# A decoder step on one core: a quarter of the first expert matrix loaded without a copy, and the residual's transposition of x taken from DRAM

## The chip, the core and the metric

The kernel runs on one core of a Trainium2 chip. The core has five engines with queues of their own: PE (TensorE, matrix products into PSUM), DVE (VectorE), ACT (ScalarE), POOL (GpSimd) and SP (SyncE, which here only issues DMAs). ACT and POOL issue DMAs too. Every DMA is served by the core's 16 DMA engines; the profile calls SP's queue q1, ACT's q10 and POOL's q0. The metric is the device time of one execution in microseconds (us), as the median of three runs.

## What is computed

The reference is one step of one layer for 256 prompt tokens and 64 sample tokens (T = 320 rows) of width D = 2048, all float32. What matters here:

```python
def layer(x, ...):
    m, ... = mixer(rmsnorm(x, norm_mix), ...)          # w_in, SSD scan, short convolution, w_out
    x = x + m                                          # x itself is needed again here
    x = x + mem_attend(rmsnorm(x, norm_mem_q), ...)
    x = x + peer(rmsnorm(x, norm_ffn), w_peer_q, sub_keys, peer_u, peer_v)

def rmsnorm(x, g):
    return x * rsqrt(mean(x * x) + EPS) * g            # a factor for each row, a gain for each column

# peer, in each block: all 16384 experts' rows of u and v are candidates
act = gelu(einsum('td,tkd->tk', xi, u[ei]))
out = einsum('tk,tkd->td', gi * act, v[ei])
```

The memory keys and values are `rmsnorm(mem) @ w_mem_k` and `@ w_mem_v`, for the prompt.

## The kernel before

**Stages.** PE's work is one long row of matrix products, stage after stage: memory keys and values (`tokens_gemm`, 8 column tiles of 16 units, lines 309 to 350), then w_in with the SSD scan worked in between (`gemm`, units of 12 products 128x320), the z part of w_in, w_out in two halves, memory attention, the retrieval scores, the first expert matrix u (`u_unit`, 128 tiles of four units) and the second, v (`v_unit`). Each weight tile is cut in a high and a low part, H and L (`split`, line 262: ACT copies to H, DVE subtracts for L), and three products of them replace one in full precision. Seven H and seven L tiles go round.

**Order of the work.** The orders on PE, ACT and DVE are those in which the program is written (`manual_schedule`); a stream (class `Stream`) runs loads, splits and products of successive units some steps apart: up to three loads ahead, and the split of a unit about six units ahead of its products. At each unit that leaves the stream ("a pop") side generators advance by a fixed rate: `strm.side(gen, rate)`. The orders on POOL and SP are set by the scheduler, which places instructions by its own estimate of when they are ready. In the expert stages POOL's order is written too.

**x for the mixer** (`norm_T`, lines 438 to 463). In the first stage a side generator (rate 0.36) loads x in three blocks of rows (128, 128, 64), takes the sum of squares on ACT, the row factor r, multiplies each row on DVE by r and by the gain, which was loaded as a broadcast tile of 1 MB (`gain_rows`), transposes four 128-column pieces at a time on PE, and splits the 512 columns into `AH` and `AL` in one ACT and one DVE instruction.

**x for the residual** (`residual`, lines 1071 to 1088). In the z part another side generator loads x again as rows (`xr`, POOL's queue), transposes it on PE in twelve groups of four, and ACT copies each group to `XF`. Beside it `short_in` (1090 to 1098) loads the short convolution's result `ys` back from DRAM on POOL's queue, 16 pieces into three buffers, and splits them into `BH` and `BL`. Behind both, POOL's queue has the first loads of memory keys, `kv` (line 1162).

**The first expert matrix.** A row of peer_u is wanted with 32-column blocks in an order that DVE's 32x32 transposition (line 2043) can use. So `ordered_rows` (586 to 597) copies peer_u in DRAM to `u_d`, 128 copies of 1 MB issued from ACT's queue in the early stages, at 0.12 and then 0.272 copies a pop; in the u stage `rows` (lines 2020 to 2025) loads a tile of 1 MB with one DMA in runs of 8 KB, into one of three rooms. A room falls free when DVE has transposed its last quarter. The same stage gathers rows of peer_u for the sample tokens, 1 MB a gather, on POOL's queue (`gu`, line 1925).

Of the kernel before, what the change touches and what calls it, by code (L numbers as in the profile page):

```python
# [11 lines left out]
F32 = mybir.dt.float32  # L12
# [3 lines left out]
AF = mybir.ActivationFunctionType  # L16
# [32 lines left out]
XW, LAG = 5, 4  # L49
AIN, AHEAD, HOT, G2B = 2, 1, 2, 3  # L50
Q_AHEAD, Q_ROOM, KV_MORE = 5, 4, 2

QA, QB = (0, 2, 4, 6, 8, 10, 12, 14, 15, 16), (0, 4, 6, 8, 9, 11, 13, 14, 15, 16)
QN = (QA, QB, QA)
# [111 lines left out]
def wait(n):  # L166
    for _ in range(n):
        yield 1
# [11 lines left out]
def step(ctx, tc, ins, outs, dbg=None, stop=None):  # L180
# [81 lines left out]
    def split(h, l, src):  # L262

        S.activation(h, src, AF.Copy)  # L264
        V.tensor_tensor(l, src, h.bitcast(F32), ALU.subtract)  # L265
# [141 lines left out]
    xh_d = drp.tile([D, TP], F32R, name="xh_d")  # L407
    xl_d = drp.tile([D, TP], F32R, name="xl_d")
    x1_d = drp.tile([P, KC, T], F32, name="x1_d")
    x2_d = drp.tile([TP, D], F32, name="x2_d")  # L410
    x2s_d = drp.tile([TS, D], F32, name="x2s_d")
    acc_d = drp.tile([P, 1024], F32, name="acc_d")
    act_d = drp.tile([P, P, TP], F32, name="act_d")
    u_d = [drp.tile([P, 4 * D], F32, name=f"u_d{i}") for i in range(P // 4)]
    g2_d = drp.tile([P, NG1 // 4, 4 * P], F32, name="g2_d")


# [12 lines left out]
    def rstd(st, n):  # L430
        V.tensor_scalar(st[:n, 1:2], st[:n, 0:1], 1.0 / D, EPS, op0=ALU.mult, op1=ALU.add)
        rsqrt(st[:n, 2:3], st[:n, 3:4], st[:n, 1:2])
        return st[:n, 2:3]
# [1 line left out]
    def tokens():  # L435
        return pM.tile([P, D], F32, tag="xt", bufs=2, name="xt")

    def norm_T(src, n, gb, h, l, cols):

        xt = tokens()  # L440
        nc.sync.dma_start(xt[:n], src)
        yield from wait(2)
        junk = pM.tile([P, D], mybir.dt.bfloat16, tag="junk", bufs=1, name="junk")
        st = pM.tile([P, 4], F32, tag="st", bufs=3, name="st")
        for i in range(2):
            half = slice(1024 * i, 1024 * i + 1024)
            S.activation(junk[:n, half], xt[:n, half], AF.Square, accum_out=st[:n, i:i + 1])
            yield 1
        V.tensor_tensor(st[:n, 0:1], st[:n, 0:1], st[:n, 1:2], ALU.add)
        r = rstd(st, n)  # L450
        yield 1
        for g in range(5):
            if g < 4:
                part = slice(512 * g, 512 * g + 512)
                V.scalar_tensor_tensor(xt[:n, part], xt[:n, part], r, gb[:n, part], ALU.mult, ALU.mult)
            if g:
                pt = ps("pt")
                for j in range(4):
                    k = 4 * g - 4 + j
                    transpose(pt[:, j * n:(j + 1) * n], xt[:n, k * P:(k + 1) * P])  # L460
                split(h[:, 4 * g - 4:4 * g, cols], l[:, 4 * g - 4:4 * g, cols],
                      pt[:, 0:4 * n].rearrange("p (j n) -> p j n", j=4))
            yield 1

    def gain_rows(g):
        gb = pM.tile([P, D], F32, tag="gb", bufs=1, name="gb")
        nc.sync.dma_start(gb, g.rearrange("(o d) -> o d", o=1).broadcast_to([P, D]))
        return gb


    gk = pM.tile([16, P], F32, name="gk")
# [43 lines left out]
    strm.side(mi, 0.75)  # L515

    def x_norm():
        yield from wait(2)
        gb = gain_rows(norm_mix[0])
        yield from wait(2)  # L520
        for b in range(2):
            yield from norm_T(x_prompt[0, b * P:(b + 1) * P], P, gb, AH, AL, slice(b * P, b * P + P))
        yield from norm_T(x_sample.rearrange("b l d -> (b l) d"), TS, gb, AH, AL, slice(TP, T))


    TRI = pX.tile([P, P], F32, name="TRI")
# [59 lines left out]
    def ordered_rows(share):  # L586
        pops = count()

        done_ = 0.0
        for i in range(P // 4):  # L590
            for b in range(4):
                while done_ < 1:
                    done_ += share[0] if next(pops) < 100 else share[1]
                    yield 1
                done_ -= 1
                nc.scalar.dma_start(u_d[i][32 * b:32 * b + 32].rearrange("p (a d) -> p a d", d=512),
                                    peer_u[0, 512 * i:512 * i + 512, 512 * b:512 * b + 512].rearrange("(a p) d -> p a d", p=32))

    strm.steady = chain(wait(36), ordered_rows((0.12, 0.272)))
    side = strm.side(chain(x_norm(), vectors(), histories()), 0.36)  # L600
    for w, dst in ((w_mem_k, p_mem_k), (w_mem_v, p_mem_v)):
        d2 = dst[0, 0].rearrange("m h d -> m (h d)")
        for c in range(4):
# [466 lines left out]

    def residual():

        xts = []
        for b in range(3):
            if b < 2:
                for src in (x_prompt[0, 0:P], x_prompt[0, P:TP]) if b == 0 else (x_sample.rearrange("b l d -> (b l) d"),):
                    xts.append(pZ.tile([P, D], F32, tag="xr", bufs=2, name="xr"))
                    nc.gpsimd.dma_start(xts[-1][:src.shape[0]], src)
                    yield 1
            n = P if b < 2 else TS  # L1080
            xt = xts[b]
            for g in range(4):
                pt = ps("pt")
                for j in range(4):
                    k = 4 * g + j
                    transpose(pt[:, j * n:(j + 1) * n], xt[:n, k * P:(k + 1) * P])
                S.activation(XF[:, 4 * g:4 * g + 4, b * P:b * P + n], pt[:, 0:4 * n].rearrange("p (j n) -> p j n", j=4), AF.Copy)
                yield 1

    def short_in():  # L1090
        ys = []
# [929 lines left out]
    def rows(i):  # L2021

        asked.append(i)
        xt = box["x", i] = wtile2()
        nc.sync.dma_start(xt, u_d[i // 4][:, D * (i % 4):D * (i % 4) + D])

    def u_unit(i, q):

# [107 lines left out]
    def sample_out():  # L2136
        tiles, gains = {}, []

        def rows_in(name, src):
            t = o4(name)[0:TS]  # L2140
            nc.gpsimd.dma_start(t, src)
            return t

        def gain_in(c):
            nc.gpsimd.dma_start(gains[c], norm_final[512 * c:512 * c + 512].rearrange("(o d) -> o d", o=1).broadcast_to([TS, 512]))

        for c in range(3):
            gains.append(pL.tile([P, 512], F32, tag="g2", bufs=G2B, name="gain")[0:TS])
            gain_in(c)
        for n in range(2 * TS + AHEAD):  # L2150
            if n < 2 * TS:
                a, j = divmod(n, TS)
                tiles[n] = o4("gv")
                nc.gpsimd.indirect_dma_start(out=tiles[n], out_offset=None, in_=V4,
                                             in_offset=bass.IndirectOffsetOnAxis(ap=EV[:, 2 * j + a:2 * j + a + 1], axis=0))
            if n >= AHEAD:
                a, j = divmod(n - AHEAD, TS)
                gv = tiles.pop(n - AHEAD)
                if j == 0:
                    V.tensor_scalar(ACC, gv, WS[:, 0:1], None, op0=ALU.mult)  # L2160
                else:
                    V.scalar_tensor_tensor(ACC, gv, WS[:, j:j + 1], ACC, ALU.mult, ALU.add)
                if j == TS - 1 and a == 0:
                    nc.gpsimd.dma_start(acc_d, ACC)
                    yield from wait(3)
            yield 1

        rate(sw, R_SUM)
        st = pL.tile([TS, 8], F32, name="st")
        halves = []  # L2170
        for a in range(2):
            x = rows_in("xs", x2s_d[:, 1024 * a:1024 * a + 1024])
            ys = [rows_in("ys", (acc_d, ACC)[a][TS * r:TS * r + TS]) for r in range(a, 2)]
            yield from wait(3)
            if a:
                V.tensor_tensor(x, x, ACC[0:TS], ALU.add)
                yield 1
            while ys:
                y = ys.pop()
                V.tensor_tensor(x, x, y, ALU.add)  # L2180
                if ys:
                    yield 1
            S.activation(y, x, AF.Square, accum_out=st[:, a:a + 1])
            del y
            halves.append(x)
            yield 1
        gains.append(o4("gain")[0:TS, 0:512])
        gain_in(3)
        ms = st[:, 2:3]
        V.tensor_tensor(ms, st[:, 0:1], st[:, 1:2], ALU.add)  # L2190
        V.tensor_scalar(ms, ms, 1.0 / D, EPS, op0=ALU.mult, op1=ALU.add)
        rsqrt(st[:, 3:4], st[:, 4:5], ms)
        yield from wait(2)
        for a, x in enumerate(halves):
            for c in range(2):
                part = slice(512 * c, 512 * c + 512)
                V.scalar_tensor_tensor(x[:, part], x[:, part], st[:, 3:4], gains[2 * a + c], ALU.mult, ALU.mult)
                yield 1
            nc.gpsimd.dma_start(y_sample.rearrange("b l d -> (b l) d")[:, 1024 * a:1024 * a + 1024], x)
# [202 lines left out]
```

## Time and profile before

| what | value |
|---|---|
| median of 3 runs | 3074.57 us (3071.89 to 3076.22) |
| profiled execution, its own time | 3074.92 us |
| its span, first to last instruction | 3073.2 us |
| PE busy | 3047.5 us, 99% |
| DVE, ACT, POOL busy | 74%, 52%, 44% |
| DMA traffic | 909.19 MB, mean 296 GB/s |

In the profile's rows a line L264 is line 264 of the program; out<-in names the tiles; x counts instructions; "<-" names what ended a wait. A pipelined product is listed with its whole passage (0.31 us for 320 columns), though the next one starts 0.15 us behind it: what a product costs PE is read from start to start.

### The profile page before, as it was taken

Reading aid. Unit: us, or ns where it says so; the run is one execution under the profiler, and the core shown is the slowest. Engines: PE = TensorE matmul, PEld = TensorE weight load, DVE = VectorE, ACT = ScalarE, POOL = GpSimd, SP = SyncE. Lnnn points to the kernel's source line nnn. Section 1 sums busy time; section 2 is a strip of 40 time slices with the busy share of each in tenths; the row PEclk is TensorE's granted clock in tenths of the full one; section 3 lists DMA queues with packets and bytes.
Section 4 is the critical chain, followed back from the end, with each engine's and each line's share of the span. In section 5 each row is a group of like instructions: output and inputs, shape, how many; then the busy total and the mean of one; then the engine's idle time right before and its main releaser. Section 6 shows DMA issues by size and latency. Waiting matters only on the chain.

```text
span 3073.2 us, 55381 instructions
## 1 busy us (share of the span) xinstructions
PE 3047.5 (99%) x19717; PEld 2792.1 (91%) x19717; DVE 2272.4 (74%) x4493; ACT 1589.3 (52%) x3207; POOL 1346.6 (44%) x1499
## 2 busy tenths in 40 slices
PE   9999999999999999999999999999999999999998
PEld 7889999999999998889999999888888888888887
DVE  6556866666565556656788899989884888878887
ACT  6544643434554444444554444776664545555555
POOL 0011221111110012310458999989886666545553
PEclk9999999999999999999999999999999999999999
DMA  8888899899999868965956888879998999999997
GB/s 284 290 277 301 301 338 331 308 327 306 359 327 345 294 186 258 258 224 162 261 201 204 302 311 317 310 285 322 333 335 257 342 325 358 337 343 325 322 328 243
DMA packets 445753, 909.19 MB, mean 296 GB/s; under 512 B 43528, under 2 KB 252576, under 8 KB 420004
## 3 DMA queue, kind: packets, MB, share of 16 engines
q1 hardware_dynamic: 316804, 543.59, 51.3%
q0 software_dynamic: 60656, 227.32, 22.3%
q10 hardware_dynamic: 68016, 134.75, 12.8%
q8 instruction: 154, 2.52, 0.3%
q14 instruction: 123, 1.01, 0.1%
HBM read 849.44 MB, written 190.05 MB: 338 GB/s over the span
## 4 chain that ended last, share of the span: by engine, by line
PE 91%; POOL 3%; issue 2%; DVE 2%; DMA 1%; ACT 0%; SPq 0%; DVEq 0%; POOLq 0%; ACTq 0%
PE pg L394 11%; PE pg L396 11%; PE pg L395 11%; PE acc L2266 7%; PE acc L2267 7%; PE acc L2265 7%; PE pu L2074 7%; PE pu L2075 4%; PE pu L2081 2%; POOL L L2055 2%; PE pu L2080 2%; PE pu L2079 2%; PE pg L341 2%; PE pg L342 2%; PE pg L343 2%
## 5 line engine op out<-in xcount | busy, mean ns | idle before, releaser
L265 DVE TENSOR_TENSOR L<-W,H 128x512 fp32r<-128x512 f32 x1309 | 902.2, 714 | 379.9 <-ACT H L264 362.8
L264 ACT ACTIVATE H<-W 128x512 fp32r<-128x512 f32 x1309 | 795.3, 628 | 678.6 <-PE acc L2267 212.5
L2055 POOL TENSOR_TENSOR L<-tt,H 128x512 fp32r<-128x512 f32 x511 | 646.9, 1298 | 65.2 <-ACT H L2052 58.4
L394 PE MATMUL pg<-AH,H 128*128 128x320 f32 x1664 | 522.3, 314 | 0.0
L396 PE MATMUL pg<-AH,L 128*128 128x320 f32 x1664 | 514.3, 309 | 0.0
L395 PE MATMUL pg<-AL,H 128*128 128x320 f32 x1664 | 514.1, 309 | 0.0
L2265 PE MATMUL acc<-H,wt 128*128 128x512 f32 x1018 | 396.2, 389 | 2.3 <-ACT H L264 2.3
L2266 PE MATMUL acc<-L,wt 128*128 128x512 f32 x1018 | 396.1, 389 | 0.2 <-DVE L L265 0.2
L2267 PE MATMUL acc<-H,wt 128*128 128x512 f32 x1018 | 396.0, 389 | 0.0
L2052 ACT ACTIVATE H<-tt 128x512 fp32r<-128x512 f32 x512 | 309.7, 627 | 141.0 <-DVE tt L2043 110.1
L2043 DVE STREAM_TRANSPOSE tt<-W 128x512 f32<-128x512 f32 x512 | 339.0, 692 | 57.3 <-POOL L L2055 54.5
L2074 PE MATMUL pu<-XP,H 128*128 128x512 f32 x1035 | 371.3, 399 | 0.4 <-ACT H L2052 0.4
L394 PEld LDWEIGHTS pg<-AH,H 128*128 128x128 f32 x1664 | 313.0, 188 | 2.0 <-issue 0.5
L395 PEld LDWEIGHTS pg<-AL,H 128*128 128x128 f32 x1664 | 312.6, 188 | 1.8
L396 PEld LDWEIGHTS pg<-AH,L 128*128 128x128 f32 x1664 | 312.3, 188 | 0.0
L2075 PE MATMUL pu<-XP,L 128*128 128x256 f32 x1104 | 297.1, 279 | 1.1 <-POOL L L2055 1.1
L2215 POOL TENSOR_TENSOR at<-at,G 128x108 f32<-128x108 f32 x192 | 160.8, 851 | 273.4 <-DMA at<-act_d 212.7
L2081 PE MATMUL pu<-XP,L 128*128 128x256 f32 x944 | 269.0, 285 | 1.7 <-POOL L L2055 1.6
L2079 PE MATMUL pu<-XP,H 128*128 128x256 f32 x944 | 267.6, 284 | 0.0
L2080 PE MATMUL pu<-XP,H 128*128 128x256 f32 x944 | 267.0, 283 | 0.0
L2074 PEld LDWEIGHTS pu<-XP,H 128*128 128x128 f32 x1035 | 194.3, 188 | 40.4 <-ACT H L2052 0.7
L2265 PEld LDWEIGHTS acc<-H,wt 128*128 128x128 f32 x1018 | 191.1, 188 | 42.8 <-ACT H L264 3.2
(533 smaller groups left out, 6110.6 us busy)
## 6 DMA issues: line engine op xcount, KB each, us to landing
u_d<-in_peer_u_dram ACTq DMA_DIRECT2D x128, 1024.0 KB
W<-u_d SPq DMA_DIRECT2D x128, 1024.0 KB
W<-in_peer_v_dram SPq DMA_DIRECT2D x256, 512.0 KB
W<-in_w_in_dram SPq DMA_DIRECT2D x176, 512.0 KB
W<-in_w_out_dram SPq DMA_DIRECT2D x64, 512.0 KB
W<-in_w_mem_k_dram SPq DMA_DIRECT2D x32, 512.0 KB
W<-in_w_mem_v_dram SPq DMA_DIRECT2D x32, 512.0 KB
W<-in_w_mem_q_dram SPq DMA_DIRECT2D x32, 512.0 KB
```

The source lines that it names most:

```text
L264: S.activation(h, src, AF.Copy)
L265: V.tensor_tensor(l, src, h.bitcast(F32), ALU.subtract)
L394: PE.matmul(out, hv[:, j, c0:c1], ah[:, k, 0:n], start=st, stop=False)
L395: PE.matmul(out, hv[:, j, c0:c1], al[:, k, 0:n], start=False, stop=False)
L396: PE.matmul(out, lv[:, j, c0:c1], ah[:, k, 0:n], start=False, stop=sp)
L2043: V.transpose(tt.rearrange("p (k a i) -> p k a i", a=4, i=32), box["x", i].rearrange("p (a k j) -> p k a j", a=4, k=16)[:, 4 * q:4 * q + 4])
L2055: G.tensor_tensor(l, src, h.bitcast(F32), ALU.subtract)
L2074: PE.matmul(*wide, start=k == 0, stop=False)
L2075: PE.matmul(pu[:, 0:TP], lv[:, j], PP["xp"][:, 0, k], start=False, stop=False)
L2265: PE.matmul(out, th, h, start=j == 0, stop=False)
L2266: PE.matmul(out, th, l, start=False, stop=False)
L2267: PE.matmul(out, tl, h, start=False, stop=j == P - 1)
```

## The change

1. **x is transposed once, raw.** `rows_T` replaces `norm_T`. It takes the same sums of squares, and sets r on a diagonal; one product of ones with that diagonal (`prr`) puts the row factors in all partitions, and ACT copies them to `R`. Then the raw rows are transposed in twelve groups of four, as before. Each group is copied by ACT to `raw` and stored to DRAM in `xT_d` by POOL's queue. One step later DVE multiplies the group by `R`, and each of its four pieces is scaled by its column's gain and split (`scaled_split`: one ACT and one DVE instruction a piece). The broadcast tile of gains goes; the gains come from `GAIN`, so `vectors()`, which fills it, is moved ahead of x.
2. **The residual loads `xT_d`** into `XF`, 16 DMAs of 160 KB on POOL's queue. Its loads of x, its 48 transpositions and its 12 copies go.
3. **A quarter of u isn't copied.** Of 32 groups of four tiles the eight in `STRAIGHT` (8, 10 to 22: 32 tiles out of 128) are left out of `ordered_rows`, whose later rate goes from 0.272 to 0.235. In the u stage each of these tiles is loaded straight from peer_u by four DMAs, each to 32 partitions in runs of 2 KB.
4. **Three small gain loads** of the sample's last norm stand later in the code.

The core of the diff:

```diff
+STRAIGHT = set(range(8, 24, 2))
...
-    def norm_T(src, n, gb, h, l, cols):
+    def rows_T(src, n, cols):
...
         r = rstd(st, n)
+        diag = pM.tile([P, P], F32, tag="diag", bufs=1, name="diag")
+        V.tensor_scalar(diag[:n, 0:n], ident[:n, 0:n], r, None, op0=ALU.mult)
+        yield 1
+        pt = ps("prr")
+        PE.matmul(pt[:, 0:n], ones[0:n], diag[:n, 0:n], start=True, stop=True)
+        R = pM.tile([P, P], F32, tag="R", bufs=2, name="R")
+        S.activation(R[:, 0:n], pt[:, 0:n], AF.Copy)
         yield 1
         for g in range(5):
+            if g:
+                xn = pM.tile([P, 4, P], F32, tag="xn", bufs=2, name="xn")[:, :, 0:n]
+                V.tensor_tensor(xn, pt[:, 0:4 * n].rearrange("p (j n) -> p j n", j=4),
+                                R[:, 0:n].unsqueeze(1).broadcast_to([P, 4, n]), ALU.mult)
+                for j in range(4):
+                    k = 4 * g - 4 + j
+                    scaled_split(AH[:, k, cols], AL[:, k, cols], xn[:, j], gain(0, k))
             if g < 4:
-                part = slice(512 * g, 512 * g + 512)
-                V.scalar_tensor_tensor(xt[:n, part], xt[:n, part], r, gb[:n, part], ALU.mult, ALU.mult)
-            if g:
                 pt = ps("pt")
                 for j in range(4):
-                    k = 4 * g - 4 + j
+                    k = 4 * g + j
                     transpose(pt[:, j * n:(j + 1) * n], xt[:n, k * P:(k + 1) * P])
-                split(h[:, 4 * g - 4:4 * g, cols], l[:, 4 * g - 4:4 * g, cols],
-                      pt[:, 0:4 * n].rearrange("p (j n) -> p j n", j=4))
+                raw = pM.tile([P, 4, P], F32, tag="raw", bufs=2, name="raw")[:, :, 0:n]
+                S.activation(raw, pt[:, 0:4 * n].rearrange("p (j n) -> p j n", j=4), AF.Copy)
+                nc.gpsimd.dma_start(xT_d[:, 4 * g:4 * g + 4, cols], raw)
...
-        for i in range(P // 4):
+        for i in sorted(set(range(P // 4)) - STRAIGHT):
...
-    strm.steady = chain(wait(36), ordered_rows((0.12, 0.272)))
-    side = strm.side(chain(x_norm(), vectors(), histories()), 0.36)
+    strm.steady = chain(wait(36), ordered_rows((0.12, 0.235)))
+    side = strm.side(chain(wait(2), vectors(), x_norm(), histories()), 0.36)
...
     def residual():
-        xts = []
-        for b in range(3):
...
-                transpose(pt[:, j * n:(j + 1) * n], xt[:n, k * P:(k + 1) * P])
-            S.activation(XF[:, 4 * g:4 * g + 4, b * P:b * P + n], ..., AF.Copy)
-            yield 1
+        for k in range(KC):
+            nc.gpsimd.dma_start(XF[:, k], xT_d[:, k])
+            yield 1
...
-        nc.sync.dma_start(xt, u_d[i // 4][:, D * (i % 4):D * (i % 4) + D])
+        if i // 4 in STRAIGHT:
+            for b in range(4):
+                nc.sync.dma_start(xt[32 * b:32 * b + 32].rearrange("p (a d) -> p a d", d=512),
+                                  U2[P * i:P * i + P, 512 * b:512 * b + 512].rearrange("(a p) d -> p a d", p=32))
+        else:
+            nc.sync.dma_start(xt, u_d[i // 4][:, D * (i % 4):D * (i % 4) + D])
...
-        for c in range(3):
-            gains.append(pL.tile([P, 512], F32, tag="g2", bufs=G2B, name="gain")[0:TS])
-            gain_in(c)
         for n in range(2 * TS + AHEAD):
+            if n in (TS, TS + 8, TS + 16):
+                gains.append(pL.tile([P, 512], F32, tag="g2", bufs=G2B, name="gain")[0:TS])
+                gain_in(len(gains) - 1)
```

The lines of the changed program stand some lines off: L264 is L265 there, L394 is L395, L1095 is L1088.

**Where it moves instructions.** On PE, in the z part, a group of four transpositions of `xr` stands between the products of two tiles twelve times. Before:

```order
L395 MATMUL pg_9074<-AL,H 128x320
L396 MATMUL pg_9074<-AH,L 128x320
L257 MATMUL pt<-ident,xr 128x128 x4
L394 MATMUL pg_9073<-AH,H 128x320
L395 MATMUL pg_9073<-AL,H 128x320
```

None of them is left there; in the first stage, whose twelve groups stay, three single products of ones with the diagonal are new:

```order
L343 MATMUL pg_485<-L,MH 128x512
L344 MATMUL pg_485<-H,ML 128x512
L457 MATMUL prr<-diag,ones 128x128
L342 MATMUL pg_484<-H,MH 128x512
L343 MATMUL pg_484<-L,MH 128x512
```

On POOL, in the z part, the queue of loads before. `ys` are the pieces of the short convolution, `xr` the rows of x, `kv` the rooms of memory keys, 256 KB a DMA:

```order
L1095 DMA ys<-ysc_d 128x320
L1078 DMA xr<-in_x_prompt_dram 128x2048
L1095 DMA ys<-ysc_d 128x320
L1078 DMA xr<-in_x_prompt_dram 128x2048
L1095 DMA ys<-ysc_d 128x320 x4
L1078 DMA xr<-in_x_sample_dram 64x2048
L1095 DMA ys<-ysc_d 128x320 x10
L1162 DMA kv_11743<-in_cache_mem_k_dram 64x4x256 x2
L1162 DMA kv_11744<-in_cache_mem_k_dram 64x4x256 x2
```

And now, from the third `ys` on:

```order
L1088 DMA ys<-ysc_d 128x320
L1080 DMA XF<-xT_d 128x320 x14
L1155 DMA kv_11779<-in_cache_mem_k_dram 64x4x256 x2
L1155 DMA kv_11780<-in_cache_mem_k_dram 64x4x256 x2
L1155 DMA kv_11781<-in_cache_mem_k_dram 64x4x256 x2
L1155 DMA kv_11782<-in_cache_mem_k_dram 64x4x256 x2
L1155 DMA kv_11783<-in_cache_mem_k_dram 64x4x256 x2
L1088 DMA ys<-ysc_d 128x320
L1155 DMA kv_11784<-in_cache_mem_k_dram 64x4x256 x2
L1155 DMA kv_11785<-in_cache_mem_k_dram 64x4x256 x2
L1088 DMA ys<-ysc_d 128x320 x12
```

The fourth `ys` stood behind two loads of x; it stands behind 16 loads of `XF` and ten of `kv` now, and all 14 loads of `kv` stand ahead of the last twelve `ys`, where they stood behind them.

On ACT, in the first stage, the splits of the first block of x before (`AH<-pt`), between those of the weights (`H<-W`):

```order
L264 ACTIVATE H<-W 128x512 x2
L264 ACTIVATE AH<-pt 128x4x128
L264 ACTIVATE H<-W 128x512 x3
L264 ACTIVATE AH<-pt 128x4x128
L264 ACTIVATE H<-W 128x512 x2
L264 ACTIVATE AH<-pt 128x4x128
```

And now:

```order
L265 ACTIVATE H<-W 128x512 x2
L475 ACTIVATE raw<-pt 128x512
L265 ACTIVATE H<-W 128x512 x3
L298 ACTIVATE AH<-xn,GAIN 128x128 x4
L475 ACTIVATE raw<-pt 128x512
L265 ACTIVATE H<-W 128x512 x2
L298 ACTIVATE AH<-xn,GAIN 128x128 x4
L475 ACTIVATE raw<-pt 128x512
```

Where one copy of 512 columns stood, there are a copy of 512 and four of 128. The three gain loads of part 4 stand at the same place of POOL's order in both programs, between the same subtractions of the u stage's last tiles.

More of the change, by code (lines that the diff above doesn't have):

```diff
@@ L409, in step @@
     x1_d = drp.tile([P, KC, T], F32, name="x1_d")
+    xT_d = drp.tile([P, KC, T], F32, name="xT_d")
     x2_d = drp.tile([TP, D], F32, name="x2_d")
@@ L413, in step @@
     act_d = drp.tile([P, P, TP], F32, name="act_d")
-    u_d = [drp.tile([P, 4 * D], F32, name=f"u_d{i}") for i in range(P // 4)]
+    u_d = [None if i in STRAIGHT else drp.tile([P, 4 * D], F32, name=f"u_d{i}") for i in range(P // 4)]
     g2_d = drp.tile([P, NG1 // 4, 4 * P], F32, name="g2_d")
@@ L450, in norm_T @@
         r = rstd(st, n)
+        diag = pM.tile([P, P], F32, tag="diag", bufs=1, name="diag")
[5 more added lines that the diff above has]
+        S.activation(R[:, 0:n], pt[:, 0:n], AF.Copy)
         yield 1
         for g in range(5):
+            if g:
[5 more added lines that the diff above has]
+                    scaled_split(AH[:, k, cols], AL[:, k, cols], xn[:, j], gain(0, k))
             if g < 4:
-                part = slice(512 * g, 512 * g + 512)
-                V.scalar_tensor_tensor(xt[:n, part], xt[:n, part], r, gb[:n, part], ALU.mult, ALU.mult)
-            if g:
                 pt = ps("pt")
                 for j in range(4):
-                    k = 4 * g - 4 + j
+                    k = 4 * g + j
                     transpose(pt[:, j * n:(j + 1) * n], xt[:n, k * P:(k + 1) * P])
-                split(h[:, 4 * g - 4:4 * g, cols], l[:, 4 * g - 4:4 * g, cols],
-                      pt[:, 0:4 * n].rearrange("p (j n) -> p j n", j=4))
+                raw = pM.tile([P, 4, P], F32, tag="raw", bufs=2, name="raw")[:, :, 0:n]
+                S.activation(raw, pt[:, 0:4 * n].rearrange("p (j n) -> p j n", j=4), AF.Copy)
+                nc.gpsimd.dma_start(xT_d[:, 4 * g:4 * g + 4, cols], raw)
             yield 1
[L465 to L468, printed above, removed]
     gk = pM.tile([16, P], F32, name="gk")
@@ L517, in x_norm @@
     def x_norm():
-        yield from wait(2)
-        gb = gain_rows(norm_mix[0])
-        yield from wait(2)
         for b in range(2):
-            yield from norm_T(x_prompt[0, b * P:(b + 1) * P], P, gb, AH, AL, slice(b * P, b * P + P))
-        yield from norm_T(x_sample.rearrange("b l d -> (b l) d"), TS, gb, AH, AL, slice(TP, T))
+            yield from rows_T(x_prompt[0, b * P:(b + 1) * P], P, slice(b * P, b * P + P))
+        yield from rows_T(x_sample.rearrange("b l d -> (b l) d"), TS, slice(TP, T))
     TRI = pX.tile([P, P], F32, name="TRI")
@@ L1071, in residual @@
     def residual():
-        xts = []
-        for b in range(3):
[L1075 to L1078, printed above, removed]
-                    yield 1
[L1080 to L1085, printed above, removed]
-                    transpose(pt[:, j * n:(j + 1) * n], xt[:n, k * P:(k + 1) * P])
-                S.activation(XF[:, 4 * g:4 * g + 4, b * P:b * P + n], pt[:, 0:4 * n].rearrange("p (j n) -> p j n", j=4), AF.Copy)
-                yield 1
+        for k in range(KC):
+            nc.gpsimd.dma_start(XF[:, k], xT_d[:, k])
+            yield 1
     def short_in():
```

## The prediction

> **What bounds the kernel now.** I read the page first, then the busy time of each engine by stage, then PE's waits.
>
> ```profile
> span 3073.2 us, 55381 instructions
> PE 3047.5 (99%) x19717; PEld 2792.1 (91%) x19717; DVE 2272.4 (74%) x4493; ACT 1589.3 (52%) x3207; POOL 1346.6 (44%) x1499
> ```
>
> ```profile
> core 0: us, PE busy (x) PEld busy (x) DVE busy (x) ACT busy (x) POOL busy (x), PEclk, DMA share, GB/s
> 8.00:200.00 192.00, 192.00 (x913) 154.20 (x911) 115.78 (x216) 109.86 (x201) 12.43 (x28) 1.00 0.88 295
> 200.00:1140.00 940.00, 939.30 (x6766) 923.01 (x6763) 605.35 (x1219) 437.18 (x851) 140.46 (x311) 1.00 0.90 308
> 1140.00:1360.00 220.00, 215.50 (x1903) 186.95 (x1902) 136.34 (x234) 91.87 (x208) 62.68 (x97) 1.00 0.88 262
> 1550.00:2340.00 790.00, 785.97 (x5597) 738.18 (x5596) 689.46 (x1622) 469.16 (x1048) 694.99 (x570) 1.00 0.82 293
> 2340.00:2400.00 60.00, 57.41 (x282) 47.68 (x282) 36.88 (x56) 30.04 (x61) 36.55 (x35) 1.00 0.84 253
> ```
>
> PE is the bound in every stage. In the first stage and all the way to 1140 us, where the change takes away copies and adds work for DVE and ACT, it is idle for 0.7 us (192.00 of 192.00, 939.30 of 940.00). Idle time inside the program is 4.5 us in memory attention, 4.0 in the u stage and 2.6 at its turn to v. The DMA engines are up to 0.90 busy there. What isn't PE's work can move the time only by making PE wait, or by ending some of those 11 us. The longest of PE's waits from 1140 to 2370 us is for POOL, not for a DMA (us in all, times, longest):
>
> ```profile
> PE pu L2081 <- POOL L L2055: 1.6, 4, 0.6
> ```
>
> **PE's own work: what goes and what comes.** The residual's transpositions stand between products; a product takes 0.147 us from start to start. The timeline of PE at one group of four pieces of 128 rows, and at one of 64 rows:
>
> ```profile
> 804.49 0.31 PE L396 MATMUL pg<-AH,L 128*128 128x320 f32 x1
> 804.64 0.60 PE L257 MATMUL pt<-ident,xr 128*128 128x128 f32 x4
> 805.00 0.39 PE L394 MATMUL pg<-AH,H 128*128 128x320 f32 x1
> 805.23 0.31 PE L395 MATMUL pg<-AL,H 128*128 128x320 f32 x1
> ```
>
> ```profile
> 861.90 0.31 PE L396 MATMUL pg<-AH,L 128*128 128x320 f32 x1
> ...
> 862.78 0.32 PE L395 MATMUL pg<-AL,H 128*128 128x320 f32 x1
> ```
>
> From the product before the group to the second behind it go 0.74 us where two steps are 0.29: the group costs 0.44, its change of operand type with it. The narrow one costs 0.88 - 0.29 = 0.59. Eight of the first and four of the second (three blocks of rows, four groups each): 8 x 0.44 + 4 x 0.59 = 5.9 us go from PE, which nothing hides.
>
> Three products of ones with a diagonal come in the first stage. No such product of 128 columns stands alone in the trace. The nearest is that with 320:
>
> ```profile
> 827.37 0.31 PE L396 MATMUL pg<-AH,L 128*128 128x320 f32 x1
> 827.52 0.70 PE L279 MATMUL prs<-acc,ones 128*128 128x320 f32 x2
> 827.82 0.56 PE L394 MATMUL pg<-AH,H 128*128 128x320 f32 x1
> 828.22 0.30 PE L395 MATMUL pg<-AL,H 128*128 128x320 f32 x1
> ```
>
> It costs 0.85 - 0.29 = 0.56 in two passes; two of the four passes of a transposition group are 0.22. I take 0.33 each, between them: 1.0 us in all (0.7 to 1.7). The first stage's twelve groups of transpositions stay. PE's work is less by 5.9 - 1.0 = 4.9 us.
>
> **First stage: more on ACT and DVE, beside PE.**
>
> ```profile
> L265 DVE TENSOR_TENSOR L<-W,H 128x512 fp32r<-128x512 f32 x133 | 88.1, 689 | 54.8 <-ACT H L264 53.3 <-DMA W<-in_w_mem_k_dram 0.9
> L264 ACT ACTIVATE H<-W 128x512 fp32r<-128x512 f32 x133 | 79.4, 626 | 43.5 <-DVE L L265 17.8 <-DMA W<-in_w_mem_k_dram 10.7 <-DMA W<-in_w_mem_v_dram 7.7
> ...
> L298 DVE SCALAR_TENSOR_TENSOR ML<-pt,GAIN,MH 128x256 fp32r<-128x256 f32 x15 | 7.2, 480 | 4.3 <-ACT MH L297 4.3
> L297 ACT ACTIVATE MH<-pt,GAIN 128x256 fp32r<-128x256 f32 x14 | 6.6, 469 | 5.6 <-DVE ML L298 5.6
> ```
>
> A step of x falls due every 1/0.36 = 2.8 pops; a pop is 192 us / 128 = 1.5, so a step is 4.2 us of PE. DVE has 2.8 x 0.69 = 1.9 for the weights, 0.69 for the product with R (by L265's row) and four pieces of 128 columns, each between 0.24 and 0.48 (half of and all of L298): 3.6 to 4.5 us. ACT has 2.8 x 0.63 + 0.63 + 4 x (0.23 to 0.47) = 3.3 to 4.3. For four steps a block both are about full, and at worst fall 1.2 us behind; splits stand six units, 9 us, ahead of PE. I take nothing. If that cover were gone, it is up to 1.2 us a block, 3.6 in all. Who waits for ACT's new wait on `prr` are the H splits behind it, as they wait behind `AH<-pt` today. `raw` has two buffers, so ACT also waits for the store two steps, 8 us, earlier. The gains' broadcast load of 1 MB goes from SP's queue; the small loads of `vectors()` come ahead of x. Zero, with the same cover.
>
> **z part: the loads on POOL's queue.** The timeline of POOL, at the third `ys` and the first `kv`:
>
> ```profile
> 790.76 0.54 POOL L1095 DMA_DIRECT2D ys<-ysc_d  x1
> ...
> 882.29 3.83 POOL L1162 DMA_DIRECT2D kv<-in_cache_mem_k_dram  x6 [8.93 <-PE pt L257]
> ```
>
> Sixteen loads of `XF` (2.6 MB) take the place of three of x (2.5 MB), and 14 of `kv` (3.7 MB), which began at 882 us, stand right behind them, ten ahead of the fourth `ys`. Behind that wait: ACT's split of it, and on ACT all H splits behind. The traffic by queue, in 8 us with x's load and in 14 us with `kv`:
>
> ```profile
> q0 software_dynamic: 373, 2.34, 70.0%
> q10 hardware_dynamic: 289, 0.59, 19.0%
> q1 hardware_dynamic: 357, 0.36, 12.9%
> ```
>
> ```profile
> q0 software_dynamic: 629, 2.08, 48.5%
> q10 hardware_dynamic: 742, 1.49, 30.4%
> q1 hardware_dynamic: 1106, 1.10, 25.5%
> ```
>
> ACT's waits for weights from 800 to 818 us, which x's load made, and its turn at the fourth piece:
>
> ```profile
> ACT H L264 <- DMA W<-in_w_in_dram: 6.8, 3, 3.0
> ```
>
> ```profile
> 816.62 0.46 ACT L264 ACTIVATE BH<-ys 128x320 fp32r<-128x320 f32 x1
> ```
>
> When all queues have work, the packets that each gets are about as many (373, 289, 357): the share goes by packet size. [...] Here q0 had 2.34 MB / 8 us = 293 GB/s with 6.3 KB a packet, and 149 GB/s with `kv`. Ahead of the fourth `ys` there are 2.6 MB of each: 9 + (9 to 18) us, from 791 us on: it is in at 809 to 818 us, and ACT comes to it at 816.6. So ACT waits 0 to 2 us there. The weights get 45 GB/s (0.36 MB / 8) and 79 (1.10 / 14) meanwhile, and need 512 KB in two units of 12 x 0.147 us: 149 GB/s. The shortage of 8 us x 104 GB/s = 0.8 MB made ACT wait 6.8 us, and PE by the table above not at all; `kv` right behind it, 3.7 MB at 149 GB/s, adds 25 us x 70 GB/s = 1.7 MB, or 11 us. ACT would be late by 18 us at worst, by 7 at best; PE's cover is six units, 10.6 us. PE waits 0 to 7 us: I take 1, near the lower end, since the copies on q10 are fewer and no `kv` follows at 882 us.
>
> **Copies and u stage.** 32 copies less are 32 MB read and written less before memory attention, where PE waits 0.7 us in all: nothing. In the u stage a straight tile is 1 MB in runs of 2 KB, not 8. From 1750 to 1950 us, and (last row) the copies in runs of 2 KB on the page:
>
> ```profile
> q1 hardware_dynamic: 9565, 39.30, 51.8%
> q0 software_dynamic: 3264, 23.86, 32.9%
> ```
>
> ```profile
> q10 hardware_dynamic: 68016, 134.75, 12.8%
> ```
>
> q1 took 0.518 x 200 / 39.3 = 2.6 us of all engines for a MB, q10 0.128 x 3073 / 134.75 = 2.9: 0.3 us more a tile. The stage's DVE row counts 260 transpositions in 400 us, 6.2 us a tile, and three rooms leave a load about two tiles, 12 us:
>
> ```profile
> L2043 DVE STREAM_TRANSPOSE tt<-W 128x512 f32<-128x512 f32 x260 | 170.2, 689 | 11.9 <-POOL L L2055 11.6
> ```
>
> DVE never waited for a tile there. SP issues four DMAs for one: about a microsecond. I take nothing. The three gain loads didn't move in POOL's order: nothing.
>
> **Sum.** -4.9 + 1 = -3.9 us on the profiled execution's 3074.92, which lies 0.35 above the median; against the median, 3074.57 - 3.9 = 3070.7 us. That is -0.13%. About 0.2%, 6.1 us, is what a measurement of this kernel can tell from no change.
>
> **Rivals.** (a) *PE waits in the z part for real.* If `XF` in its 1280-byte runs moves at half of x's rate, its 18 us cost the weights 18 x 104 GB/s = 1.9 MB and `kv` another 1.7: 3.6 MB, 24 us at 149 GB/s. PE waits for what is over 10.6: 14 us. The time is 3074.6 - 4.9 + 14 = 3084. ACT's wait for the fourth `ys`, in at 791 + 18 + 18 = 827 us then, lies inside it. It makes the kernel slower by over 0.2% from a lateness of 21.6 us on (10.6 + 4.9 + 6.1). Against it: q0 got the most of all queues in both rows. Chance 0.08. (b) *Straight tiles come late.* By equal packets a tile's 2 KB against a gather's 7.3 KB (23.86 MB / 3264) has 21% of the engines while a gather runs, where 8 KB had about half. One gather (2.8 us a MB by its row) and the tile are 5.7 us of work, under 12; two queued gathers and a store of gates are about 11. If a quarter of the 32 tiles came 2 us late, PE would lose 16: 3086 us. Chance 0.05. [...] (c) *Lighter DMA and earlier `kv` end waits.* If half of the 11.1 us of idle time goes: 3074.6 - 4.9 - 5.5 = 3064 us. Against it: the longest wait there is for POOL. Chance 0.22. (d) *The change doesn't do what it says:* the three gain loads don't, at no price; the rest does by the order.
>
> **Chances and range.** The forecast has 0.65, with 0.04 of it under 3068.4. Faster: 0.22 + 0.04 = 0.26. Slower: 0.06 of (a) and 0.04 of (b), which may also be small: 0.10. The rest, 0.64, lies within 0.2%. The range goes from 3065 (most of (c), and the cheap end of `prr`) to 3078 (7 us of waiting in the z part, and run-to-run spread); beyond lie some 0.1 on either side.
>
> **What would show it.** Right: no `xr` rows, PE's busy time about 5 us less, idle time in the z part from 780 to 900 us of at most a few us, no DVE wait for a u tile between 1750 and 2150. Wrong: a wait of ACT's `BH` for `ys`, and behind it PE's for H, around 815 to 835 us; DVE waiting for `in_peer_u` tiles; idle time in the first stage; or the idle time in memory attention and the u stage falling by several us, by which (c) would be it.

## The result and the profile after

The changed kernel takes 3096.38 us (median of 6 runs, 3090.18 to 3100.83), the kernel before in the same comparison 3073.49 (6 runs, 3071.89 to 3076.22): a ratio of 1.0073, 95% interval 1.0063 to 1.0083. It is 22.9 us slower, where the forecast was 3.9 us faster, and lies 18 us above the top of the range. The profiled run took 3098.09 us with a span of 3096.3.

The page of the changed kernel, its span and the row of engines:

```profile
span 3096.3 us, 55537 instructions
PE 3054.2 (99%) x19675; PEld 2796.5 (90%) x19675; DVE 2270.1 (73%) x4532; ACT 1598.5 (52%) x3246; POOL 1335.5 (43%) x1524
```

PE has fewer instructions than before (19675, not 19717) and yet is busy for 6.7 us longer: some of its products were slow, as the granted clock shows below. The same stretches as before (PE's busy time stands first after the length):

```profile
8.00:200.00 192.00, 191.64 (x899) 154.18 (x901) 120.95 (x255) 121.40 (x252) 19.72 (x36) 1.00 0.90 303
200.00:1140.00 940.00, 929.70 (x6655) 911.85 (x6648) 599.34 (x1206) 429.81 (x830) 138.58 (x317) 0.99 0.81 270
1140.00:1360.00 220.00, 215.35 (x1890) 186.84 (x1889) 134.11 (x235) 90.84 (x204) 68.69 (x107) 0.99 0.87 252
1550.00:2340.00 790.00, 777.99 (x5555) 731.66 (x5554) 679.40 (x1629) 463.32 (x1039) 675.70 (x555) 1.00 0.87 287
```

PE is idle for 10.3 us between 200 and 1140 where it was idle for 0.7, and for 12.0 in the u stage where it was 4.0. The first of these lies in the z part. Windows of it; the third column from the right is the granted clock:

```profile
780.00:820.00 40.00, 40.00 (x275) 40.00 (x274) 18.06 (x32) 14.37 (x24) 22.73 (x41) 1.00 0.99 335
820.00:840.00 20.00, 12.98 (x57) 11.98 (x56) 4.45 (x8) 5.02 (x11) 4.05 (x7) 0.74 1.05 306
840.00:860.00 20.00, 17.97 (x121) 17.58 (x121) 17.95 (x33) 13.54 (x25) 1.82 (x4) 1.00 1.02 356
```

The same instruction of PE can be found in both traces by its place in the order. How late it starts in the changed kernel, in us:

| place | before | after | late by |
|---|---|---|---|
| end of the first stage (first `pdt`) | 195.60 | 197.02 | 1.4 |
| first `ptf` | 325.46 | 329.27 | 3.8 |
| z part: first `prs` | 827.52 | 843.82 | 16.3 |
| first product with BH | 907.21 | 919.42 | 12.2 |
| first product of the u stage | 1570.65 | 1584.37 | 13.7 |
| DVE's `tt` of tile 32 | 1752.58 | 1766.42 | 13.9 |
| DVE's `tt` of tile 72 | 1992.39 | 2019.34 | 27.0 |
| DVE's `tt` of tile 120 | 2306.20 | 2333.16 | 27.0 |
| last product of v | 3063.63 | 3086.53 | 22.9 |

So there are two main losses. The z part loses 14 us before the removed transpositions give some back, and tiles 32 to 71 of the u stage lose 13. Behind tile 120 the changed kernel gains 4.1 us on this one trace of the kernel before. The traces of all the other kernels below gain 1.9 to 4.3 us there too, those with only one of the two parts included, so neither part is the cause.

What PE and ACT waited for in the z part, from 785 to 880 us (in all, times, longest):

```profile
ACT H L265 <- DMA W<-in_w_in_dram: 33.2, 8, 8.6
...
PE pg L395 <- ACT H L265: 6.9, 2, 4.4
...
PE prs L280 <- DVE acc L294: 2.0, 1, 2.0
```

The weights come late, ACT's splits with them, and PE runs out of splits. It isn't the fourth `ys`: no wait for it is in the list. What the queues moved meanwhile, first from 793 to 809 us (`XF`), then from 813 to 833 (`kv`); weights are q1, copies q10:

```profile
q0 software_dynamic: 849, 2.94, 46.3%
q10 hardware_dynamic: 920, 1.85, 30.0%
q1 hardware_dynamic: 1598, 1.59, 28.3%
```

```profile
q0 software_dynamic: 1053, 3.48, 66.9%
q1 hardware_dynamic: 1085, 1.08, 22.3%
q10 hardware_dynamic: 543, 1.08, 16.1%
```

The weights need 149 GB/s. They got 1.59 MB / 16 us = 99 in the first stretch and 1.08 / 20 = 54 in the second, where the kernel before gave them 2.91 / 20 = 146 from 813 to 833 us. They fall short by 0.8 and 1.9 MB, 18 us at their own rate. The timeline of PE then shows something that the list of waits does not:

```profile
827.10 0.64 PE L395 MATMUL pg<-AH,H 128*128 128x320 f32 x1 [4.42 <-ACT H L265]
...
832.52 0.47 PE L396 MATMUL pg<-AL,H 128*128 128x320 f32 x1
832.79 0.47 PE L397 MATMUL pg<-AH,L 128*128 128x320 f32 x1
...
833.28 0.31 PE L396 MATMUL pg<-AL,H 128*128 128x320 f32 x1
833.42 0.30 PE L397 MATMUL pg<-AH,L 128*128 128x320 f32 x1
```

For 5.5 us behind the wait, products start 0.27 us apart, not 0.147; the granted clock explains it:

```profile
828.00:832.00 4.00, 4.00 (x17) 4.00 (x17) 0.44 (x1) 0.00 (x0) 0.55 (x1) 0.50 1.06 221
```

Twenty-one products there and twelve behind the second wait cost 0.12 us more each, 4.0 us, which counts as busy. Waits of 8.9 us and about 4.0 of slow clock are 12.9 of the 14.

In the u stage, DVE's waits from 1550 to 2340 us have a row that the kernel before did not have, and PE's longest wait grew with it:

```profile
DVE tt L2041 <- DMA W<-in_peer_u_dram: 21.9, 10, 5.9
```

```profile
PE pu L2079 <- POOL L L2053: 8.9, 11, 2.0
```

The queues while a straight tile loads (1773 to 1778 us, between gathers):

```profile
q1 hardware_dynamic: 651, 1.07, 100.8%
q0 software_dynamic: 8, 0.04, 4.2%
```

Here q1 alone fills all 16 engines and moves 1.07 MB in 5 us, 214 GB/s; loads of the copied tiles from 1750 to 1950 us in the kernel before took 2.6 us of all engines a MB, 380 GB/s. Over a whole straight group (1766 to 1795) the two queues need 101% of the engines; over the same group before (1752 to 1776), 89%:

```profile
q1 hardware_dynamic: 2388, 5.31, 68.9%
q0 software_dynamic: 433, 3.15, 32.1%
```

```profile
q1 hardware_dynamic: 1177, 4.84, 51.8%
q0 software_dynamic: 432, 3.15, 37.2%
```

### The profile page after: what moved, and what is told of

It is laid out like the page before. It is cut to its first block, busy times and chain, and to the rows that moved or that the text cites. A ratio compares the mean times of both kernels' runs of the same rounds, so it can differ in the third digit from the quotient of the medians.

```text
span 3096.3 us, 55537 instructions
## 1 busy us (share of the span) xinstructions
PE 3054.2 (99%) x19675; PEld 2796.5 (90%) x19675; DVE 2270.1 (73%) x4532; ACT 1598.5 (52%) x3246; POOL 1335.5 (43%) x1524
## 4 chain that ended last, share of the span: by engine, by line
PE 87%; DMA 6%; DVE 4%; POOL 1%; issue 1%; ACT 1%; SPq 0%; DVEq 0%; POOLq 0%; ACTq 0%
PE pg L395 11%; PE pg L396 11%; PE pg L397 11%; PE acc L2263 7%; PE acc L2265 7%; PE acc L2264 7%; PE pu L2072 7%; PE pu L2073 4%; DMA W<-in_peer_u_dram 3%; PE pg L342 2%; PE pg L344 2%; PE pg L343 2%; PE pgate L1970 2%; PE pu L2079 2%; PE pu L2077 2%; PE pu L2078 2%
## 5 line engine op out<-in xcount | busy, mean ns | idle before, releaser
L265 ACT ACTIVATE H<-W 128x512 fp32r<-128x512 f32 x1309 | 794.6, 628 | 688.3 <-PE pg L396 230.2
L395 PE MATMUL pg<-AH,H 128*128 128x320 f32 x1664 | 524.0, 315 | 6.9 <-ACT H L265 6.9
L395 PEld LDWEIGHTS pg<-AH,H 128*128 128x128 f32 x1664 | 315.2, 189 | 9.1 <-ACT H L265 7.4
L2213 POOL TENSOR_TENSOR at<-at,G 128x108 f32<-128x108 f32 x192 | 141.0, 747 | 294.3 <-DMA at<-act_d 244.7
```

What stands on the lines that cost most here:

```text
L395: PE.matmul(out, hv[:, j, c0:c1], ah[:, k, 0:n], start=st, stop=False)
```

## The experiments

Each is an edit of the changed kernel unless said otherwise.

**Which part costs what.** No straight tiles:

```diff
-STRAIGHT = set(range(8, 24, 2))
+STRAIGHT = set()
-    strm.steady = chain(wait(36), ordered_rows((0.12, 0.235)))
+    strm.steady = chain(wait(36), ordered_rows((0.12, 0.272)))
```

> The changed kernel without the straight tiles: all 32 row groups of the first expert matrix are copied again, at the old rate; x's single transposition and its spill stay. Theory: of the 22.9 us that the changed kernel lost, the trace puts 13.3 on the straight tiles in the u stage and the rest on the first stages (3.8), the z part (8.4 net) and memory attention (1.5). So this one comes out 11 to 14 us below the changed kernel, at 3082 to 3086 us, with PE's waits for H from 820 to 845 us still there, since the kv loads still stand ahead of the ys loads. Rival: the straight tiles only pass on a lateness that the z part made, and the loss is all x's; then it stays at 3094 us or above.

Measured 3084.82 us (3083.74 to 3088.08), 1.0039 of the kernel before (1.0026 to 1.0052): 11.6 less than the changed kernel. The u stage loses nothing. The z part loses 13.1 us between the first `ptf` and the first `prs`; in the changed kernel it was 12.5.

The opposite, the kernel before with the straight tiles alone (`STRAIGHT`, the loads of L2020 and the rate 0.235):

> The kernel before with nothing but the straight tiles and the lower rate of copies. Theory: DVE waits for W in the groups of straight tiles that meet gathers, 13 us in all, and the turn to v gives up to 2 back: 3085 to 3087 us. The z part shows no wait of PE. Rival: the tiles come late only because the x part moved the gathers against them; then 3074 to 3077 us.

Measured 3089.89 us (3086.39 to 3094.25), 1.0056 (1.0043 to 1.0069), 3 above what I expected. Tiles 32 to 71 lose 15.1 us here, and PE never waits in the z part. So each part loses without the other. In the profiled runs the two losses add up: at the last product of v they are 8.4 and 14.4 us, and 22.9 in the changed kernel. The medians, with 11.8 and 16.8 us against 22.9, do so only within their intervals.

**Why straight tiles are late.** The same bytes, runs and number of DMAs, written to 128 partitions:

```diff
-            for b in range(4):
-                nc.sync.dma_start(xt[32 * b:32 * b + 32].rearrange("p (a d) -> p a d", d=512),
-                                  U2[P * i:P * i + P, 512 * b:512 * b + 512].rearrange("(a p) d -> p a d", p=32))
+            for a in range(4):
+                nc.sync.dma_start(xt[:, 512 * a:512 * a + 512], U2[P * i:P * i + P, 512 * a:512 * a + 512])
```

> The changed kernel with each straight tile's four DMAs cut along the columns: each fills all 128 partitions with runs of 2 KB, instead of 32 partitions with four runs each. (The rows then lie in W in another arrangement than the products need, so the values of these tiles' products are others; bytes, runs, number of DMAs and all instructions stay.) Theory 1, the place where they are written: in the changed kernel a 2-KB packet took 145 to 162 ns in the straight groups and 84 ns where 2-KB runs go to 128 partitions, and the four DMAs moved 200 to 220 GB/s with all engines busy. Then the packets fall to 84 to 110 ns here, the tile to about 3 us of all engines, and the u stage's 13 us go: 3082 to 3086 us. Theory 2, the share by packet: 2-KB runs lose against gathers wherever they are written; 3094 us or above. Theory 3, the issue: each DMA on SP's queue waits for the one eight before it, and a straight tile makes five with its store of activations; also 3094 us or above.

Measured 3085.55 us (3083.84 to 3086.28), 1.0037 (1.0024 to 1.0050). From tile 32 to tile 72 it loses no time at all. The same five microseconds of its trace:

```profile
q1 hardware_dynamic: 1147, 1.87, 101.9%
q0 software_dynamic: 7, 0.06, 3.4%
```

It moves 1.87 MB, 374 GB/s, where the changed kernel moved 1.07. Only the place in SBUF differs, so the share by packets, the size of the DMAs and their number on SP are not the cause. What SP showed in the changed kernel was an effect: its DMAs, which go round eight semaphores in this trace, waited 17.6 us in all for earlier tiles' DMAs to finish, 15 times, since those were slow:

```profile
SPq L2020 <- DMA W<-in_peer_u_dram: 17.6, 15, 5.6
```

In the wide version this row is gone. Three rows of q1 over tiles 33 to 95 give the price (packets, MB, share of the engines): before in 371 us, changed in 384, wide in 371.

```profile
q1 hardware_dynamic: 17591, 71.61, 51.9%
```

```profile
q1 hardware_dynamic: 30902, 72.11, 64.9%
```

```profile
q1 hardware_dynamic: 30565, 71.61, 54.5%
```

That is 192.5, 249.2 and 202.2 us of all engines. With 30 straight tiles in each of the last two, one costs 0.3 us more than a copied one when written to 128 partitions, and 1.9 more when written to 32 at a time.

Then 64 partitions with two runs each, two DMAs for each half:

```diff
+            for b in range(4):
+                nc.sync.dma_start(xt[64 * (b // 2):64 * (b // 2) + 64, 1024 * (b % 2):1024 * (b % 2) + 1024].rearrange("p (a d) -> p a d", d=512),
+                                  U2[P * i:P * i + P, 512 * b:512 * b + 512].rearrange("(a p) d -> p a d", p=64))
```

> The changed kernel with each straight tile's DMA filling 64 partitions with two runs of 2 KB each (two DMAs for the lower half, two for the upper), instead of 32 with four. (The rows lie in another arrangement, so these tiles' products have other values; bytes, runs and DMAs stay.) In the runs so far a 2-KB packet of such tiles took 150 ns to 32 partitions and 84 ns to 128. [...] Rival, the rate goes with the number of partitions: packets of 84 to 110 ns, the u stage loses 2 us or less, 3083 to 3087 us.

Measured 3097.86 us (3096.62 to 3101.29), 1.0078 (1.0061 to 1.0095), with 20.9 us of waits of DVE for W. Sixty-four partitions are no better than 32 in time (3096.38), and the rival is refuted. From tile 33 to 95, in 382 us here, q1 took 244.9 us of all engines, beside 249.2 with 32 partitions and 202.2 with 128:

```profile
q1 hardware_dynamic: 30869, 71.71, 64.1%
```

The blocks of 32 partitions in the order 0, 2, 1, 3:

```diff
-            for b in range(4):
+            for b in (0, 2, 1, 3):
```

> The changed kernel with the four DMAs of a straight tile in the order 0, 2, 1, 3 of its blocks of 32 partitions; everything else as it is, the values too. If the DMAs of SP's queue overlap at all, two that follow each other now go to the lower and the upper half of the partitions. Theory 1, they are worked off one after the other: packets stay at about 150 ns, 3094 to 3098 us. Theory 2, each engine has two in hand, and the halves don't hinder each other: packets of 85 to 120 ns, and half or more of the u stage's 13 us goes: 3083 to 3090 us.

Measured 3095.47 us (3085.57 to 3097.51), 1.0060 (1.0040 to 1.0080). Neither theory holds cleanly. In the profiled run DVE's waits for W fell from 21.9 to 10.8 us, and tiles 32 to 71 lost 6.0 us instead of 13.1; the median hardly moved. This one trace hints that DMAs that follow each other overlap a little; the runs spread too far to show it, or what it is worth.

**What straight tiles collide with.** These two, and the first of the next part, have kv behind ys (below). Four groups straight where no gather runs:

```diff
+STRAIGHT = {1, 2, 3, 4}
+    strm.steady = chain(wait(36), ordered_rows((0.12, 0.254)))
```

> As the one with both repairs, but with four groups (16 tiles) loaded straight where no gather runs yet: groups 1 to 4 instead of 8, 10 to 22. Theory: a straight tile costs 5.2 us of all DMA engines instead of 2.6 to 3, and only together with gathers (8.5 to 9 us a group) is that more than the 24 us that a group takes; without gathers a group has 14 + 6 = 20 us of work in 23.5, and nothing is lost: within 2 us of the kernel with both repairs. Rival: a straight tile is late by itself, by its four DMAs or their issue on SP; then 16 tiles lose half of what 32 lost, 6 to 8 us more.

Measured 3069.80 us (3067.33 to 3073.51), 0.4 above the kernel with both repairs. In the first of these groups (1583 to 1608 us) q1 takes 93.7% of the engines, and PE is busy for all of its 25 us:

```profile
q1 hardware_dynamic: 3298, 5.42, 93.7%
```

```profile
1583.00:1608.00 25.00, 25.00 (x212) 25.00 (x211) 23.75 (x113) 11.03 (x21) 22.82 (x19) 1.00 0.95 219
```

One tile in four straight, beside the gathers (all copies are made, those of these tiles not used):

```diff
+STRAIGHT = set()
-        if i // 4 in STRAIGHT:
+        if 32 <= i < 96 and i % 4 == 1:
```

> As the one with both repairs (all groups copied), but the second tile of each group from 8 to 23 is loaded straight, beside the gathers: 16 straight tiles, never two in a row (their copies are made, and not used). Theory of the DMA engines' capacity: a group had 21 to 21.6 us of DMA work in 24 to 26; one straight tile adds 2.4 and it still fits: 0 to 3 us more than the kernel with both repairs. Rival: a straight tile beside gathers costs the same wherever it stands, 13.3 / 32 = 0.42 us each: 6 to 7 us more.

Measured 3069.36 us (3068.59 to 3073.99), the median of the kernel with both repairs; the trace loses 1.2 us in tiles 32 to 71. The two runs fit the theory that the same dear tile is free while its group's DMA fits into the group's time. How full the engines are doesn't tell alone which group loses. In the changed kernel they are full in all eight straight groups (96 to 104% by q1 and q0). The first, third, fourth and fifth take 27 to 30 us, where they took 21 to 26 before, and become longer by 5.3, 5.5, 1.4 and 3.2 us. The other four take the 22 to 29 us that they took before and lose nothing.

**The z part.** Padded pieces of the short convolution, so that the `kv` rooms lie on them and wait:

```diff
-                ys.append(pZ.tile([P, T], F32, tag="ys", bufs=3, name="ys"))
+                ys.append(pZ.tile([P, 1684], F32, tag="ys", bufs=3, name="ys")[:, 0:T])
```

> The changed kernel with the rooms of ys padded, so that the kv rooms lie on them and POOL's queue has all ys loads ahead of the kv loads, as before the change; the 16 loads of XF stay where they are. Theory: the 14 kv loads right behind XF keep the weights at 50 to 57 GB/s from 813 to 833 us; without them the shortage that XF makes is 0.8 MB and lies inside ACT's lead, PE's waits there (4.4, 2.4, 2.0 us) and the slow clock behind them go, and the time is 3082 to 3085 us. Rival: XF's loads alone use up the lead, and the waits stay, at least half of them: 3089 us or above.

In the kernel before, the first `kv` load waited for a transposition of `xr` (`<-PE pt L257`, at 882 us): with `xr` gone, nothing held it back.

Measured 3087.55 us (3079.20 to 3091.07), 1.0040 (1.0028 to 1.0052), 3 above what I expected. The z part did as the theory says. PE has no wait and no slow clock there:

```profile
820.00:840.00 20.00, 20.00 (x136) 19.84 (x136) 15.74 (x30) 14.01 (x27) 1.61 (x3) 1.00 0.99 336
```

and the weights got 3.31 MB from 813 to 833 us instead of 1.08:

```profile
q1 hardware_dynamic: 3337, 3.31, 47.6%
```

Its first product with BH is 3.6 us earlier than before the change. What exceeds my number is the straight tiles, which lose 15.9 us in this run.

Without straight tiles, `XF` on ACT's queue, so that `kv` alone is in front of `ys`:

```diff
-            nc.gpsimd.dma_start(XF[:, k], xT_d[:, k])
+            nc.scalar.dma_start(XF[:, k], xT_d[:, k])
```

> The kernel without straight tiles (3084.8 us) with the 16 XF loads on ACT's queue, behind the copies and paced with the products, instead of POOL's; the 14 kv loads still stand ahead of all but three ys loads. Theory: kv alone is enough to starve the weights: 3.7 MB at about 165 GB/s are 22 us in which the weights get some 55 of the 149 GB/s that they need; short by 2.1 MB, or 14 us, against a lead of 10.6: PE waits 2 to 6 us, with the slow clock behind it, and the time is 3074 to 3080 us. Rival 1: it takes XF and kv together; no wait, 3068 to 3072 us. Rival 2: XF has no part in it at all, and nothing is won: 3083 us or above.

Measured 3080.37 us (3076.16 to 3081.76), 1.0016 (1.0007 to 1.0025), at the upper edge. PE waits 3.4 us in the norm's product and 3.3 for H; without straight tiles and with `XF` in front too, they were 1.8 and 8.4. `kv` ahead of `ys` on POOL's queue is enough without `XF` there, and `XF` adds to it.

**Both repairs.** kv behind ys, and no straight tiles at the old rate of copies:

> The two repairs together: kv loads behind all ys loads (padded ys), and no straight tiles (all row groups copied at the old rate). What is left of the change is x's single transposition and its spill. Theory: the padded kernel began the products with BH 3.6 us ahead of the kernel before, and the kernel without straight tiles lost nothing in the u stage; together 3068 to 3072 us, below the kernel before by 1 to 5. Rival: kv loads that come later make memory attention or its projection wait, or the copies at the old rate take the weights' share again in the z part; 3075 us or above.

Measured 3069.39 us (11 runs, 3067.36 to 3073.60) against 3074.18 of the kernel before (33 runs): 0.9986, interval 0.9977 to 0.9995. It is faster than both kernels, by 4.8 us than the kernel before. The rival was that late `kv` loads cost something later. They now start at 880.94 us:

```profile
880.94 3.72 POOL L1155 DMA_DIRECT2D kv<-in_cache_mem_k_dram  x6 [10.15 <-DVE BL L266]
```

At the first product of attention this kernel's trace is 3.9 us ahead of the trace of the kernel before, and at the last product of v 7.9. The 3.9 come from the z part, behind which it was 5.0. Of the rest, 3.8 come behind tile 120, where every other trace gains on that one trace too: its first products of v wait 2.6 us, those of the others 0.5 to 1.5. That is about half of the 3.8; the other half stays open. The profiled run is also the fastest of its eleven (3067.36 us), and the medians are 4.8 apart.

## Why the prediction was wrong

**PE's own work: right.** In the kernel with both repairs PE is 0.96 us late at the first `ptf` and 4.96 ahead at the first product with BH: 5.9 us, the number that I summed from groups of transpositions. PE is busy for 3041.4 us there, 6.1 less than before. The first stage cost 0.9 to 1.8 us in the kernels with the single transposition, where I had 1.0 for `prr`:

```profile
L457 PE MATMUL prr<-diag,ones x6: 272/274/320, 56.7 to 144.7; 128*128 128x128 f32 x4, 64*128 64x64 f32 x2
```

ACT and DVE had the cover there that I gave them: PE is idle for 0.36 us from 8 to 200 us. Of the lateness between 197 and 329 us, 0.9 comes with the rate 0.235 (it is in the kernel with the straight tiles alone) and 1.5 is a slow clock, told at the end.

**z part: the mechanism was right, the value chosen was wrong.** The step that failed is "PE waits 0 to 7 us: I take 1, near the lower end, since the copies on q10 are fewer and no `kv` follows at 882 us". My worst case, ACT late by 18 us, was what the trace shows (0.8 and 1.9 MB short), and PE waited 6.9 us for H: the upper bound. I had no row for `XF` and took x's rate, 293 GB/s; q0 moved 2.94 MB / 16 us = 184 with it, between that and the half of it that rival (a) supposed. Fewer copies did not help, because q10 had work all the same: 1.85 MB in those 16 us. The reading "the packets that each gets are about as many" rests on one stretch; the prediction's other one (629, 742 and 1106) and the two above (849, 920 and 1598; 1053, 543 and 1085) don't bear it out.

Beyond the bound came what I had not priced: 4.0 us of slow clock behind the waits, and 2.0 for the norm's product. Rival (a) said 14 us and 3084; without straight tiles it was 3084.8. The number is partly luck: its 14 us were all waits for weights, from 3.6 MB; the changed kernel's trace has 2.7 MB short, and 6.9 us of waits for H beside 2.0 for the norm's product and 4.0 of slow clock. Still, its chance of 0.08 was too low. Two rows gave me a range for q0's rate, and I took the fast end for one load and gave the slow end a few per cent.

The `kv` loads are themselves dear: each DMA fills 64 partitions, as those of the straight tiles did in the version with two runs each, and q0 took 66.9% of the engines for 20 us to move 3.48 MB, 3.8 us a MB. For x it was 70.0% of 8 us for 2.34 MB, 2.4 us a MB; the prediction's row with `kv` (48.5% of 14 us for 2.08 MB) already had 3.3. No run fills the `kv` rooms 128 partitions at a time, so how much of the z part's loss comes from this is open.

**u stage: the price was wrong.** The step that failed is "0.3 us more a tile". It was worked out from copies in runs of 2 KB, which go from DRAM to DRAM and write to no partition. It holds where the runs go to 128 partitions, and it is 1.9 us where they go to 32. I priced the length of the run, and not where it is written, though the diff shows `xt[32 * b:32 * b + 32]`. "DVE never waited for a tile there" and "I take nothing" then failed as well: DVE waited 21.9 us. A load did have some 12 us, but the first straight group's DMA had only about a tenth of its time free before, and four dear tiles in a row, with gathers, fill the engines for longer than the group took. An issue on SP took 0.32 us in the kernel before (L2025, 128 of them), so the microsecond for three more was right.

**Rival (b)** named nearly the right loss (16 us) for a wrong reason. Equal packets beside gathers are there in the wide version too, as are four small DMAs instead of one, and it loses nothing from tile 32 to tile 72; such a tile took 0.3 us more of all engines than one in a single DMA. The prediction's "about 11" us for two gathers and a store isn't made of its rows: 2.8 for each gather and 2.9 for the tile are 8.5 before the store. Together, the two rivals come to -4.9 + 14 + 16 = +25 us. That this is near the measured 22.9 is luck in part, for the reasons given. I gave each a few per cent and never both.

**Rival (c)**, lighter DMA, is refuted: with tiles loaded straight at no loss, 3085.55 us, 32 copies fewer are worth nothing against 3084.82 with all of them. The copies were hidden; taking them away won nothing.

## What to carry to other kernels

Price a DMA by the partitions that it writes too: 2-KB runs to 32 partitions at a time moved 214 GB/s here, to 128 partitions 374, and 64 gave no better time than 32. When a change frees memory, look at which later loads lay on it: they may start at once and stand in front of something small that matters, on a queue that then takes the weights' share. A load that hides today's DMA is judged by the sum over its stretch too, against the time that the stretch has (29 us of DMA work in a group of 24), and not only by one tile's lead.

## What the runs showed of the hardware

After waits of 4.4 and 2.4 us PE ran at a granted clock of 0.5 for 5.5 and 3 us: the slow clock cost 4.0 us beside 6.9 of waiting. Between 215 and 219 us the clock was also low in the changed kernel, behind a wait of 0.56 us that the kernel before has as well (0.57) without it:

```profile
215.00:219.00 4.00, 4.00 (x19) 3.59 (x19) 1.64 (x7) 2.03 (x7) 0.00 (x0) 0.57 0.45 131
```

That cost 1.5 us in this run and is missing in others of the same instructions. With `kv` behind `ys`, PE does 29 products in these 4 us, not 19, and ten at 0.147 us are the 1.5:

```profile
215.00:219.00 4.00, 4.00 (x29) 3.44 (x29) 2.06 (x9) 2.03 (x7) 0.00 (x0) 1.00 0.45 131
```

In the changed kernel the granted clock is 0.50 from 215.4 to 218.8 us, 826.4 to 833.2, 836.6 to 840.0, 1181.4 to 1184.8 (1.5 us lost in memory attention) and 1891.3 to 1894.7. In this trace each change of it lies 3.413 us, or a multiple of it, behind the one before. The waits of PE at these places were 0.56, 4.4, 2.4, 1.9 and 2.0 us. The length of a wait alone doesn't decide whether the clock falls: behind the 2.0 us for the norm's product, which ended at 843.8 us, it stayed at 1.00:

```profile
844.00:848.00 4.00, 4.00 (x27) 3.84 (x27) 3.07 (x4) 3.42 (x6) 0.00 (x0) 1.00 1.06 376
```

Behind the wait of 0.56 us come seven pairs of small products, from 213.5 to 215.3, and the clock falls 1.9 us after the first of them starts. In the trace of the kernel before, the clock changes only at 11.14 and 3066.07 us, 895 times 3.413 us apart; counted on from the first in such steps, one would fall 0.4 us after the start of the same products. That the position of the steps against the program decides whether the short pause costs anything is an estimate of mine from these two traces.
